# HGRN level products on two halves of the array, 64 keys by 64 queries each

## The chip, the cores and the metric

The kernel runs on one core of one Trainium2 chip. The metric is device time in microseconds of one execution, the median of several. Three runs of the kernel before took 3020.35, 3021.91 and 3026.28 us.

## The reference

One layer of a two-branch sequence model on 1024 latent tokens and 256 context tokens, width 2048, all in float32. A projection `u = h @ w_in` feeds two groups of heads; the change is in group A, a gated linear recurrence in both directions (HGRN2) with 8 heads of 128 key and 128 value dimensions:

```python
# one direction, one chunk; b = cumsum(log f) inside the chunk
o_inter = einsum('bhtk,bhkv->bhtv', qc * exp(b), s)
diff = b[:, :, :, None, :] - b[:, :, None, :, :]
decay = exp(where(mask, diff, -inf))
scores = einsum('bhtk,bhsk,bhtsk->bhts', qc, kc, decay)
o = o_inter + einsum('bhts,bhsv->bhtv', scores, vc)
s_new = exp(b_last)[..., None] * s + einsum('bhsk,bhsv->bhkv', kc * exp(b_last - b), vc)
```

A score of a query t and a key s carries the product of the gates f between the two, another one for each of the 128 key dimensions. The sum of both directions goes through an RMS norm and a gate, is joined with group B (an mLSTM), projected with `w_out`, added to the stream and normalised.

## The kernel before

The program goes through a prelude (modulation of the context), the context, the mLSTM heads, the eight HGRN heads and the output projection. Throughout, TensorE works on projections: a weight tile is brought in by SyncE's queue (`wraw`), split into a rounded part (`whi`, ScalarE, L209) and the rest (`wlo`, VectorE, L210), and multiplied in three matmuls (`mm3`, L218 to L220 or L222 to L224) of operands of the rounded type. `unit_a` makes one projection of 128 channels for 1024 tokens: 96 matmuls of 128 x 512. Between pieces of twelve matmuls it calls `tick()`, which advances side generators: the work of the heads is issued there, in between.

For a head, `hgrn_head` runs five projections (query, two gates, value, output gate). After the third it starts `levels_gen` as a side generator; the sixteen ticks of the last two projections advance it. The tokens of a head lie in 8 chunks of 128. `qq`, `kk` and `ff` hold queries, keys and gate products of both directions, two variants side by side, as 128 partitions (key dimension) by 1024 tokens. The scores `sc` of a chunk, 128 keys by 128 queries, are built by level. First comes one product of all keys and queries (L1101). Then for level lv = 0 to 6, with B = 2^lv, the pairs whose tokens lie in the two halves of the same block of 2B get their score from the product of decayed keys `kms` and decayed queries (L1120), and a predicated copy with the mask of the level (L1133) puts it over what `sc` holds. After the product of a level VectorE multiplies keys (L1124), queries (L1129) and gates (L1132) on to the next level, and ScalarE gathers the next key operand (`kmix`, L1085).

In the kernel before, the work of a level is issued for each half of the chunks (g = 0, 1) at a tick of its own: four matmuls of 128 keys by 128 queries into one PSUM bank (tag `mx`, three banks), then the products and the predicated copy of 128 x 512. All engines run their instructions in program order; a matmul waits for `kms` and `qq`, VectorE's query product waits for the matmuls that read the queries, the predicated copy for the bank. `hout_gen` uses `sc` later, in the projections of the next head.

Of the kernel before, what the change touches and what calls it, by code (L numbers as in the profile page):

```python
# [9 lines left out]
F32 = mybir.dt.float32  # L10
F32R = mybir.dt.float32r
U8 = mybir.dt.uint8
# [9 lines left out]
P = 128  # L22
# [12 lines left out]
def view(t, off, dims):  # L35
    return bass.AP(t.tensor, t.offset + off, [list(t.ap[0])] + [list(d) for d in dims])


class Body:
# [957 lines left out]

    def phase_hgrn(self):
        nc, mp = self.nc, self.mp
        self.lvl = mp.tile([P, 7, P], U8, name="lvl")  # L1000
        lf = mp.tile([P, 7, P], F32, tag="h_sc", name="lvl_f")
        nc.gpsimd.dma_start(out=lf, in_=self.a["k_lvl"])
        nc.gpsimd.tensor_copy(out=self.lvl, in_=lf)
        self.tail = None
        for h in range(HH):
            self.hgrn_head(h)
        self.finish(self.tail)
# [66 lines left out]
    def levels_gen(self, st):  # L1074
        nc, mp = self.nc, self.mp
        V = nc.vector
        T = NT
        qq, kk, ff = st["qq"], st["kk"], st["ff"]
        sc = mp.tile([P, T], F32, tag="h_sc", name=self.nm("h_sc"))
        st["sc"] = sc  # L1080

        def kmix(lv, g):
            B = 1 << lv
            km = mp.tile([P, 512], F32, tag="h_t2", bufs=3, name=self.nm("h_km"))
            nc.scalar.copy(view(km, 0, [[2 * B, 512 // (2 * B)], [B, 2], [1, B]]),  # L1085
                           view(kk, g * 512, [[2 * B, 512 // (2 * B)], [T + B, 2], [1, B]]))
            return km

        kss = []
        for g in range(2):  # L1090
            s = slice(g * 512, (g + 1) * 512)
            ks = mp.tile([P, 512], F32, tag="h_t1", bufs=2, name=self.nm("h_ks"))
            V.tensor_tensor(out=ks, in0=kk[:, 0, s], in1=kk[:, 1, s], op=ALU.add)
            kss.append(ks)
        yield
        pts = []
        for g in range(2):
            pt = self.mx()
            for c in range(4):
                cc = (g * 4 + c) * P  # L1100
                nc.tensor.matmul(pt[:, c * P:(c + 1) * P], kss[g][:, c * P:(c + 1) * P], qq[:, 0, cc:cc + P],  # L1101
                                 start=True, stop=True)
            pts.append(pt)
        kms = [kmix(0, g) for g in range(2)]
        for g in range(2):
            s = slice(g * 512, (g + 1) * 512)
            nc.scalar.copy(sc[:, s], pts[g])
            V.tensor_tensor(out=qq[:, 1, s], in0=qq[:, 0, s], in1=ff[:, 1, s], op=ALU.mult)
            V.tensor_tensor(out=qq[:, 0, s], in0=qq[:, 0, s], in1=ff[:, 0, s], op=ALU.mult)
        yield  # L1110
        for lv in range(7):
            B = 1 << lv
            dims = [[2 * B, P // (2 * B)], [T + B, 2], [1, B]]
            np_ = 512 // (2 * B)
            dimg = [[2 * B, np_], [T + B, 2], [1, B]]
            for g in range(2):
                o = g * 512
                pt = self.mx()
                for c in range(4):
                    nc.tensor.matmul(pt[:, c * P:(c + 1) * P], kms[g][:, c * P:(c + 1) * P],  # L1120
                                     view(qq, o + c * P, dims), start=True, stop=True)
                fk = view(ff, o + T + B, [[2 * B, np_], [-(T + B), 2], [0, B]])
                kv = view(kk, o, dimg)
                V.tensor_tensor(out=kv, in0=kv, in1=fk, op=ALU.mult)  # L1124
                if lv < 6:
                    kms[g] = kmix(lv + 1, g)
                fq = view(ff, o + B, [[2 * B, np_], [T - B, 2], [0, B]])
                qv = view(qq, o, dimg)
                V.tensor_tensor(out=qv, in0=qv, in1=fq, op=ALU.mult)  # L1129
                fe = view(ff, o, [[T, 2], [2 * B, np_]])  # L1130
                fo = view(ff, o + B, [[T, 2], [2 * B, np_]])
                V.tensor_tensor(out=fe, in0=fe, in1=fo, op=ALU.mult)  # L1132
                V.copy_predicated(out=sc[:, o:o + 512].rearrange("p (c t) -> p c t", t=P),  # L1133
                                  mask=view(self.lvl, lv * P, [[0, 4], [1, P]]),
                                  data=pt.rearrange("p (c t) -> p c t", t=P))
                yield

        for d, g in ((0, 0), (1, 1), (0, 1), (1, 0)):
            pt = self.mx()
            for c in range(4):  # L1140
                cc = (g * 4 + c) * P
                nc.tensor.transpose(pt[:, c * P:(c + 1) * P], kk[:, d, cc:cc + P], self.ident)
            nc.scalar.copy(kk[:, d, g * 512:(g + 1) * 512], pt)
            if (d, g) == (1, 1):
                yield
# [176 lines left out]
def constants():  # L1322
    ident = np.eye(P, dtype=np.float32)
    s = np.arange(P)[:, None]
    t = np.arange(P)[None, :]
    lvl = np.stack([((s // (2 * B) == t // (2 * B)) & (s // B != t // B)) for B in (1, 2, 4, 8, 16, 32, 64)],
                   axis=1).astype(np.float32)
    mb = np.stack([np.where(s <= t, 0.0, -1e30), np.where(s >= t, 0.0, -1e30)], axis=1).astype(np.float32)
    comb = np.zeros((4, 2), np.float32)
    comb[0:2, 0] = 1.0  # L1330
    comb[2:4, 1] = 1.0
    sel = np.zeros((32, 2, 64), np.float32)
    for i in range(2):
        for d in range(2):
            for r in range(4):
                sel[(i * 2 + d) * 4 + r, i, d * 32 + r] = 1.0
                sel[16 + (i * 2 + d) * 4 + r, i, d * 32 + r] = 1.0
    return {"k_ident": ident, "k_lvl": lvl, "k_mbias": mb, "k_comb": comb, "k_sel": sel}


def body(tc, nc, **a):
    Body(tc, nc, a).run()


_CONST = constants()
_SHAPES = {"x": (NT, D), "c": (1, D), "ctx": (NC, D), "c_ctx": (D,), "w_mod": (D, 3 * D), "b_mod": (1, 3 * D),
           "w_in": (D, N_IN), "conv_w": (1, 3, 3, D), "conv_b": (1, D), "hg_lb": (2, 2, 1024),
# [21 lines left out]
```

## Time and profile before

| | |
|---|---|
| median of three runs | 3021.91 us |
| the profiled execution | 3019.23 us |
| its span, first to last instruction | 3017.4 us |
| mean granted TensorE clock | 0.990 |
| TensorE matmul busy | 2918.0 us, 97% |
| VectorE, ScalarE busy | 1676.7 us (56%), 970.7 us (32%) |
| product before the levels, first and second head | at 1605.05 and 1742.44 us, 137.4 us apart |

Busy time of an engine is time in which at least one of its instructions runs. A matmul's duration in the trace reaches from its start to the modelled end of its results, so matmuls in a row overlap in the list: what one costs is read from one start to the next. PEld is the load of a matmul's weights, listed apart. The chain of waits is followed back from the last instruction and says what each stretch of the time went to.

### The profile page before, as it was taken

Reading aid. Unit: us, or ns where it says so; the run is one execution under the profiler, and the core shown is the slowest. Engines: PE = TensorE matmul, PEld = TensorE weight load, DVE = VectorE, ACT = ScalarE, POOL = GpSimd, SP = SyncE. Lnnn points to the kernel's source line nnn. Section 1 sums busy time; section 2 is a strip of 40 time slices with the busy share of each in tenths; the row PEclk is TensorE's granted clock in tenths of the full one; section 3 lists DMA queues with packets and bytes.
Section 4 is the critical chain, followed back from the end, with each engine's and each line's share of the span. In section 5 each row is a group of like instructions: output and inputs, shape, how many; then the busy total and the mean of one; then the engine's idle time right before and its main releaser. Section 6 shows DMA issues by size and latency. Waiting matters only on the chain.

```text
span 3017.4 us, 41425 instructions
## 1 busy us (share of the span) xinstructions
PE 2918.0 (97%) x16265; PEld 2502.6 (83%) x16265; DVE 1676.7 (56%) x3154; ACT 970.7 (32%) x1650; POOL 366.0 (12%) x549
## 2 busy tenths in 40 slices
PE   6999998999999999999999999999999999999998
PEld 3689976987897797889778888888888888899876
DVE  7876657563835656383535363544445363634776
ACT  5664545342233223223312222222222232322332
POOL 1011111031012103201210101001010101310111
PEclk9999999999999999999999999999999999999999
DMA  9855642123322323322241112121111212753685
GB/s 321 276 167 169 187 136 68 47 57 106 84 62 72 112 70 79 111 79 75 62 114 42 52 35 58 37 56 51 42 52 42 55 38 58 224 190 118 216 310 178
DMA packets 331843, 325.13 MB, mean 108 GB/s; under 512 B 16512, under 2 KB 285072, under 8 KB 329600
## 3 DMA queue, kind: packets, MB, share of 16 engines
q1 hardware_dynamic: 296848, 243.04, 27.3%
q0 software_dynamic: 30368, 69.52, 8.0%
q10 hardware_dynamic: 4432, 9.91, 0.9%
q8 instruction: 128, 2.10, 0.3%
q14 instruction: 67, 0.55, 0.1%
HBM read 289.37 MB, written 33.05 MB: 107 GB/s over the span
## 4 chain that ended last, share of the span: by engine, by line
PE 75%; DMA 10%; DVE 8%; issue 3%; ACT 2%; POOL 2%; SPq 0%; ACTq 0%; DVEq 0%; POOLq 0%
PE pj L220 16%; PE pj L219 16%; PE pj L218 16%; PE pj L223 5%; PE pj L224 5%; PE pj L222 5%; PE mx L1120 3%; DMA wraw<-in_w_in_dram 2%; DMA am_raw<-in_w_mod_dram 2%; DVE wlo L210 2%; DVE m_acc L855 1%; PE mx L944 1%; DMA m_gt<-d_oz 1%; PE mx L949 1%; PE mx L1162 1%
## 5 line engine op out<-in xcount | busy, mean ns | idle before, releaser
L218 PE MATMUL pj<-hh,whi 128*128 128x512 f32 x2304 | 927.8, 403 | 1.0 <-ACT m_pad L777 1.0
L220 PE MATMUL pj<-hh,wlo 128*128 128x512 f32 x2304 | 902.5, 392 | 6.7 <-DVE wlo L210 6.7
L219 PE MATMUL pj<-hl,whi 128*128 128x512 f32 x2304 | 901.9, 391 | 0.0
L210 DVE TENSOR_TENSOR wlo<-wraw,whi 128x512 fp32r<-128x512 f32 x556 | 391.1, 708 | 664.7 <-ACT whi L209 605.2
L209 ACT CAST whi<-wraw 128x512 fp32r<-128x512 f32 x556 | 340.8, 619 | 889.6 <-PE pj L219 599.9
L220 PEld LDWEIGHTS pj<-hh,wlo 128*128 128x128 f32 x2304 | 434.0, 188 | 102.7 <-DVE wlo L210 10.5
L218 PEld LDWEIGHTS pj<-hh,whi 128*128 128x128 f32 x2304 | 434.6, 189 | 89.0 <-issue 2.5
L219 PEld LDWEIGHTS pj<-hl,whi 128*128 128x128 f32 x2304 | 434.9, 189 | 84.4
L222 PE MATMUL pj<-whi,yh 128*128 128x256 f32 (+1 forms) x768 | 245.9, 320 | 4.4 <-DVE res L1247 4.4
L223 PE MATMUL pj<-wlo,yh 128*128 128x256 f32 (+1 forms) x768 | 246.3, 321 | 2.8 <-DVE wlo L210 2.7
L224 PE MATMUL pj<-whi,yl 128*128 128x256 f32 (+1 forms) x768 | 246.0, 320 | 0.0
L855 DVE SCALAR_TENSOR_TENSOR m_acc<-m_pad,cwt,m_acc 128x512 f32<-128x512 f32 x256 | 184.1, 746 | 3.0
L222 PEld LDWEIGHTS pj<-whi,yh 128*128 128x128 f32 x768 | 147.4, 192 | 14.9 <-DVE res L1247 4.8
L223 PEld LDWEIGHTS pj<-wlo,yh 128*128 128x128 f32 x768 | 147.3, 192 | 13.5 <-DVE wlo L210 3.2
L224 PEld LDWEIGHTS pj<-whi,yl 128*128 128x128 f32 x768 | 147.5, 192 | 10.0
L222 PE MATMUL pj<-whi,hh 128*128 128x256 f32 x512 | 147.4, 289 | 2.0 <-ACT m_pad L777 2.0
L223 PE MATMUL pj<-wlo,hh 128*128 128x256 f32 x512 | 145.8, 285 | 1.4 <-DVE wlo L210 1.4
L224 PE MATMUL pj<-whi,hl 128*128 128x256 f32 x512 | 145.5, 284 | 0.0
L1085 ACT COPY h_km<-h_kk 128x512 f32<-128x512 f32 x112 | 74.5, 665 | 207.1 <-DVE h_kk L1124 147.1
L1120 PEld LDWEIGHTS mx<-h_qq,h_km 128*128 128x128 f32 x896 | 123.6, 191 | 9.3
L1120 PE MATMUL mx<-h_qq,h_km 128*128 128x128 f32 x896 | 126.4, 284 | 0.0
L1193 POOL TENSOR_TENSOR h_ss<-h_ss,nhalf 128x4 f32<-128x4 f32 x16 | 16.6, 1036 | 858.2 <-DVE h_ss L1192 858.2
(308 smaller groups left out, 4340.6 us busy)
## 6 DMA issues: line engine op xcount, KB each, us to landing
wraw<-in_w_in_dram SPq DMA_DIRECT2D x230, 512.0 KB, 3.8
wraw<-in_w_out_dram SPq DMA_DIRECT2D x96, 512.0 KB, 4.7
am_raw<-in_w_mod_dram SPq DMA_DIRECT2D x128, 256.0 KB, 5.9
wraw<-in_w_mod_dram SPq DMA_DIRECT2D x32, 512.0 KB, 3.6
d_y<-yhl POOLq DMA_DIRECT2D x64, 256.0 KB, 3.6
wraw<-in_w_in_dram SPq DMA_DIRECT2D x32, 256.0 KB, 5.9
xt<-in_x_dram SPq DMA_DIRECT2D x8, 1024.0 KB, 6.6
m_bc<-d_rows POOLq DMA_DIRECT2D x64, 128.0 KB, 3.4
```

The lines of the kernel that those rows point to most:

```text
L209: nc.scalar.copy(hi, r)
L210: nc.vector.tensor_tensor(out=lo, in0=r, in1=hi.bitcast(F32), op=ALU.subtract)
L218: mm(o, hi, xh, start=start, stop=False, skip_group_check=True)
L219: mm(o, hi, xl, start=False, stop=False, skip_group_check=True)
L220: mm(o, lo, xh, start=False, stop=stop, skip_group_check=True)
L222: mm(o, xh, hi, start=start, stop=False, skip_group_check=True)
L223: mm(o, xh, lo, start=False, stop=False, skip_group_check=True)
L224: mm(o, xl, hi, start=False, stop=stop, skip_group_check=True)
L855: V.scalar_tensor_tensor(out=acc, in0=src, scalar=wc, in1=acc, op0=ALU.mult, op1=ALU.add)
L944: nc.tensor.matmul(po[:, 0:257], qs[:, j, :], cn[d][:, j, :], start=False, stop=(j == 1))
L1085: nc.scalar.copy(view(km, 0, [[2 * B, 512 // (2 * B)], [B, 2], [1, B]]), view(kk, g * 512, [[2 * B, 512 // (2 * B)], [T + B, 2], [1, B]]))
L1120: nc.tensor.matmul(pt[:, c * P:(c + 1) * P], kms[g][:, c * P:(c + 1) * P], view(qq, o + c * P, dims), start=True, stop=True)
```

## The change

The products of a level are made on two halves of TensorE's columns. Each half holds 64 of a chunk's 128 keys as weights (columns 0 to 63 and 64 to 127, results in PSUM partitions 0 to 63 and 64 to 127) and is fed only the 64 queries that its keys can meet: those of the same half of the chunk up to level 5, at level 6 those of the other half. Both groups of chunks are issued at one tick, 16 matmuls into one bank, and the generator then yields for two ticks. The results are compact: 8 chunks of 64 columns. Levels 0 to 5 are collected in `scd`, 128 x 512, with one predicated copy a level in place of two; after level 5 ScalarE copies its two halves into the diagonal blocks of `sc`, and at level 6 it copies the two off-diagonal blocks out of PSUM. The mask has six levels of 64 columns.

```diff
-        self.lvl = mp.tile([P, 7, P], U8, name="lvl")
+        self.lvl = mp.tile([P, 6, 64], U8, name="lvl")
...
+        TW, NQ = 64, 2
+        scd = mp.tile([P, 8, TW], F32, tag="h_scd", name=self.nm("h_scd"))
+        s3 = sc.rearrange("p (c t) -> p c t", t=P)
+
+        def tiles(kms, rhs, n):
+
+            pt = self.mx()
+            p3 = pt[:, 0:8 * n].rearrange("p (c t) -> p c t", t=n)
+            for c in range(8):
+                cc = (c % 4) * P
+                for j in range(NQ):
+                    q0 = j * TW
+                    nc.tensor.matmul(p3[q0:q0 + TW, c, :], kms[c // 4][:, cc + q0:cc + q0 + TW], rhs(c * P, j),
+                                     start=True, stop=True, skip_group_check=True)
+            return p3
...
-        pts = []
-        for g in range(2):
-            pt = self.mx()
-            for c in range(4):
-                cc = (g * 4 + c) * P
-                nc.tensor.matmul(pt[:, c * P:(c + 1) * P], kss[g][:, c * P:(c + 1) * P], qq[:, 0, cc:cc + P],
-                                 start=True, stop=True)
-            pts.append(pt)
+        p3 = tiles(kss, lambda o, j: qq[:, 0, o + j * TW:o + (j + 1) * TW], TW)
+        nc.scalar.copy(scd, p3)
...
-            nc.scalar.copy(sc[:, s], pts[g])
...
+            if 2 * B <= TW:
+
+                p3 = tiles(kms, lambda o, j: view(qq, o + j * TW, [[2 * B, TW // (2 * B)], [T + B, 2], [1, B]]), TW)
+            else:
+
+                def other(o, j):
+                    t = (j * TW // B ^ 1) * B
+                    return view(qq, o + t + (T if t & B else 0), [[1, B]])
+
+                p3 = tiles(kms, other, B)
             for g in range(2):
                 o = g * 512
-                pt = self.mx()
-                for c in range(4):
-                    nc.tensor.matmul(pt[:, c * P:(c + 1) * P], kms[g][:, c * P:(c + 1) * P],
-                                     view(qq, o + c * P, dims), start=True, stop=True)
...
-                V.copy_predicated(out=sc[:, o:o + 512].rearrange("p (c t) -> p c t", t=P),
-                                  mask=view(self.lvl, lv * P, [[0, 4], [1, P]]),
-                                  data=pt.rearrange("p (c t) -> p c t", t=P))
-                yield
+            if 2 * B <= TW:
+                V.copy_predicated(out=scd, mask=view(self.lvl, lv * TW, [[0, 8], [1, TW]]), data=p3)
+            else:
+                for q0 in range(0, P, B):
+                    t = q0 ^ B
+                    nc.scalar.copy(s3[q0:q0 + B, :, t:t + B], p3[q0:q0 + B])
+            if 2 * B == TW:
+                for q0 in range(0, P, TW):
+                    nc.scalar.copy(s3[q0:q0 + TW, :, q0:q0 + TW], scd[q0:q0 + TW])
+            yield 2
```

TensorE's row at level 0 of the first head, before: `mx` is a bank, `h_km` the key operand of one group of chunks, `pj` the bank of a projection; "x4" are four matmuls, one a chunk.

```order
L220 MATMUL pj_14177<-hh_4687,wlo_14181 128x512
L1120 MATMUL mx_14249<-h_qq_13893,h_km_14227 128x128 x4
L218 MATMUL pj_14177<-hh_4688,whi_14184 128x512
...
L220 MATMUL pj_14177<-hh_4689,wlo_14185 128x512
L1120 MATMUL mx_14272<-h_qq_13893,h_km_14229 128x128 x4
L218 MATMUL pj_14176<-hh_1667,whi_14285 128x512
```

The same place now; L1101 is the matmul in `tiles`, whatever the level.

```order
L220 MATMUL pj_14177<-hh_4687,wlo_14181 128x512
L1101 MATMUL mx_14256<-h_qq_13893,h_km_14236 64x64 x8
L1101 MATMUL mx_14256<-h_qq_13893,h_km_14238 64x64 x8
L218 MATMUL pj_14177<-hh_4688,whi_14184 128x512
...
L220 MATMUL pj_14176<-hh_1668,wlo_14299 128x512
L1101 MATMUL mx_14318<-h_qq_13893,h_km_14274 64x64 x8
```

Both groups of a level stand together, 16 matmuls, and 24 of a projection lie between one level and the next, where twelve lay between the groups.

VectorE's row at level 0 of that head, before: `wlo` is the split of a weight, `h_ff` the gates, `h_kk` the keys.

```order
L1129 TENSOR_TENSOR h_qq_13893<-h_qq_13893,h_ff_13895 128x256x2
L1133 COPY_PREDICATED h_sc_14200<-lvl,mx_14249 128x512
L1132 TENSOR_TENSOR h_ff_13895<-h_ff_13895 128x2x256
L1124 TENSOR_TENSOR h_kk_13894<-h_kk_13894,h_ff_13895 128x256x2
L210 TENSOR_TENSOR wlo_14398<-wraw_14395,whi_14397 128x512
L1129 TENSOR_TENSOR h_qq_13893<-h_qq_13893,h_ff_13895 128x256x2
L1133 COPY_PREDICATED h_sc_14200<-lvl,mx_14272 128x512
L1132 TENSOR_TENSOR h_ff_13895<-h_ff_13895 128x2x256
```

And now (L1143 is the query product, L1138 the key product, L1146 the gates).

```order
L1143 TENSOR_TENSOR h_qq_13893<-h_qq_13893,h_ff_13895 128x256x2
L1148 COPY_PREDICATED h_scd_14201<-lvl,mx_14256 128x512
L1146 TENSOR_TENSOR h_ff_13895<-h_ff_13895 128x2x256
L1138 TENSOR_TENSOR h_kk_13894<-h_kk_13894,h_ff_13895 128x256x2
L1143 TENSOR_TENSOR h_qq_13893<-h_qq_13893,h_ff_13895 128x256x2
L210 TENSOR_TENSOR wlo_14423<-wraw_14420,whi_14422 128x512
L1146 TENSOR_TENSOR h_ff_13895<-h_ff_13895 128x2x256
```

One predicated copy is left, behind the first query product; the second query product no longer stands behind a weight split.

## Rows read from the trace of the kernel before

**Rows 1.** The page: busy time, share of the span and instructions of each engine.

```profile
PE 2918.0 (97%) x16265; PEld 2502.6 (83%) x16265; DVE 1676.7 (56%) x3154; ACT 970.7 (32%) x1650; POOL 366.0 (12%) x549
```

**Rows 2.** One head: window, length, busy PE, PEld, DVE, ACT, POOL, granted clock, DMA.

```profile
1742.40:1879.80 137.40, 137.39 (x723) 117.83 (x722) 64.26 (x114) 34.64 (x70) 8.02 (x10) 1.00 0.18 47
```

**Rows 3.** Chain of waits, that head: shares; start, length, line, passes.

```profile
by line: PE pj L220 26.7%; PE pj L218 26.5%; PE pj L219 26.5%; PE mx L1120 9.8%; PE mx L1162 2.6%; PE mx L1142 1.5%; PE mx L1101 1.4%; PE mx L1180 1.3%; PE mx L1181 1.3%; PE mx L1182 1.3%; PE mx L1071 0.6%; PE mx L1201 0.6%; issue 0.0%
...
1742.20 0.23 PE pj L220
1742.44 1.79 PE mx L1101 x16
...
1746.98 1.33 PE mx L1120 x8
...
1755.14 0.97 PE mx L1120 x8
...
1762.54 0.89 PE mx L1120 x8
```

**Rows 4.** Timeline, one burst of level 2: start, length, engine, line.

```profile
2040.98 1.09 PEld L1120 LDWEIGHTS mx<-h_qq,h_km 128*128 128x128 f32 x8
2041.21 1.06 PE L1120 MATMUL mx<-h_qq,h_km 128*128 128x128 f32 x8
```

**Rows 5.** Timeline, the loads of L568's transposes, 64 moving columns.

```profile
512.85 1.01 PEld L568 LDWEIGHTS mx<-ident,g 64*128 64x128 f32 x15 [2.86 <-issue]
```

**Rows 6.** The instructions of L568: duration ns min/median/max, first and last start, form.

```profile
L568 PEld LDWEIGHTS mx<-ident,g x24: 134/140/222, 512.9 to 514.6; 64*128 64x128 f32 x24
```

**Rows 7.** Timeline, TensorE around L493 (32 rows by 64 columns).

```profile
159.08 0.28 PE L219 MATMUL pj<-ctl,whi 128*128 128x256 f32 x1
159.29 1.07 PE L493 MATMUL mx<-g_sb,selg 32*64 32x256 f32 x4
...
160.52 0.28 PE L218 MATMUL pj<-cth,whi 128*128 128x256 f32 x1
```

**Rows 8.** Timeline, TensorE around L413 (128 rows by one column).

```profile
807.29 0.28 PE L223 MATMUL pj<-wlo,hh 128*128 128x256 f32 x1
807.41 0.28 PE L224 MATMUL pj<-whi,hl 128*128 128x256 f32 x1
807.62 0.59 PE L413 MATMUL mx<-gate_acc,ones 128*1 128x256 f32 x2
...
808.36 0.28 PE L223 MATMUL pj<-wlo,hh 128*128 128x256 f32 x1
```

**Rows 9.** Timeline, TensorE from full width to 32 columns, rounded type.

```profile
45.58 0.28 PE L222 MATMUL pj<-whi,cth 128*128 128x256 f32 x1
45.70 0.28 PE L347 MATMUL pj<-cth,wg 128*32 128x256 f32 x1
```

**Rows 10.** Groups by line and form: count, then busy us and mean ns of one.

```profile
L413 PE MATMUL mx<-gate_acc,ones 128*1 128x256 f32 x16 | 4.7, 377 | 1.3 <-DVE m_gt L975 1.3
...
L1120 PEld LDWEIGHTS mx<-h_qq,h_km 128*128 128x128 f32 x896 | 123.6, 191 | 9.3
L577 PEld LDWEIGHTS pj<-hh,wg 128*32 128x32 f32 x32 | 3.6, 113 | 4.9 <-ACT hh L453 1.9 <-issue 0.3
```

**Rows 11.** Timeline, VectorE at level 0.

```profile
2023.12 1.15 DVE L1129 TENSOR_TENSOR h_qq<-h_qq,h_ff 128x512 f32<-128x512 f32 x1 [0.16 <-PE mx L1120]
2024.12 0.73 DVE L1133 COPY_PREDICATED h_sc<-lvl,mx 128x512 f32<-128x512 uint8 x1
2024.75 0.67 DVE L1132 TENSOR_TENSOR h_ff<-h_ff 128x512 f32<-128x512 f32 x1
2025.45 1.16 DVE L1124 TENSOR_TENSOR h_kk<-h_kk,h_ff 128x512 f32<-128x512 f32 x1
2026.46 0.67 DVE L210 TENSOR_TENSOR wlo<-wraw,whi 128x512 fp32r<-128x512 f32 x1
2027.20 1.16 DVE L1129 TENSOR_TENSOR h_qq<-h_qq,h_ff 128x512 f32<-128x512 f32 x1
```

More of the change, by code (lines that the diff above doesn't have):

```diff
@@ L999, in phase_hgrn @@
         nc, mp = self.nc, self.mp
-        self.lvl = mp.tile([P, 7, P], U8, name="lvl")
-        lf = mp.tile([P, 7, P], F32, tag="h_sc", name="lvl_f")
+        self.lvl = mp.tile([P, 6, 64], U8, name="lvl")
+        lf = mp.tile([P, 6, 64], F32, tag="h_sc", name="lvl_f")
         nc.gpsimd.dma_start(out=lf, in_=self.a["k_lvl"])
@@ L1112, in levels_gen @@
             B = 1 << lv
-            dims = [[2 * B, P // (2 * B)], [T + B, 2], [1, B]]
             np_ = 512 // (2 * B)
             dimg = [[2 * B, np_], [T + B, 2], [1, B]]
+            if 2 * B <= TW:
[5 more added lines that the diff above has]
+                p3 = tiles(kms, other, B)
             for g in range(2):
                 o = g * 512
-                pt = self.mx()
-                for c in range(4):
-                    nc.tensor.matmul(pt[:, c * P:(c + 1) * P], kms[g][:, c * P:(c + 1) * P],
-                                     view(qq, o + c * P, dims), start=True, stop=True)
                 fk = view(ff, o + T + B, [[2 * B, np_], [-(T + B), 2], [0, B]])
@@ L1325, in constants @@
     t = np.arange(P)[None, :]
-    lvl = np.stack([((s // (2 * B) == t // (2 * B)) & (s // B != t // B)) for B in (1, 2, 4, 8, 16, 32, 64)],
+    s0, t0 = s % 64, t[:, 0:64]
+    lvl = np.stack([((s0 // (2 * B) == t0 // (2 * B)) & (s0 // B != t0 // B)) for B in (1, 2, 4, 8, 16, 32)],
                    axis=1).astype(np.float32)
```

## The prediction

> **What bounds the kernel now.** I read the page first: TensorE is busy for 97% of the span [rows 1]. Then the busy time by window for one head of the HGRN phase: in 137.40 us TensorE is busy for 137.39, VectorE for 64.3, ScalarE for 34.6, at a granted clock of 1.00 [rows 2]. Then the chain of waits over the same head: it holds TensorE lines alone, and "issue" has 0.0% [rows 3]. So in this phase every microsecond of TensorE is a microsecond of the kernel, and one that VectorE or ScalarE saves is worth nothing. The chain gives the price of what is changed. A burst of eight passes of the level products costs 1.33 us at level 0, 0.97 at level 1 and 0.89 from level 2 on; the sixteen passes of the product before the levels cost 1.79 [rows 3]. (A float32 matmul runs as two passes: fourteen bursts of four instructions a head are 448, and the trace has 896 [rows 10].) With two bursts a level one head pays 1.79 + 2 x 1.33 + 2 x 0.97 + 10 x 0.89 = 15.29 us, eight heads 122 us, 4% of the span. That is all the change can touch on the path.
>
> **The change part by part.** *Passes.* A burst now holds 16 matmuls, that is 32 passes, of 64 weight columns and 64 moving columns, where the two bursts of a level held 16 passes of 128 and 128. Sixteen passes stand on each half of the array. What such a pass takes is bounded by the 64-column transposes of L568: fifteen loads, one before each, in 1.01 us, the last one 0.14 long, so (1.01 - 0.14) / 14 = 0.062 us from one to the next [rows 5, 6]; against 0.89 / 8 = 0.111 for the present pass [rows 3]. One step of 64 columns is therefore a little dearer than half. What decides is whether a step holds one pass or two.
>
> If one (the halves take turns), an ordinary burst is 32 x 0.062 = 1.98 us, dearer than the 1.78 of the two bursts that it replaces. If two: in one half the second pass of a matmul has to follow its first, but it can stand beside the first pass of the other half, so 32 passes take 17 steps, 17 x 0.062 = 1.05 us. Level 0 reads its queries element by element and pays 1.33 / 8 = 0.166 a pass, half of that 0.083: 2.66 us by turns, 1.41 side by side. Level 1 (0.97 / 8 / 2 = 0.061) goes as an ordinary one.
>
> I take two passes a step. No row of this trace has two matmuls in different columns, so the number of steps is an inference; the price of one step comes from the row in either case. What speaks for it: a load and a stream that share all rows of the array already run side by side (eight loads from 2040.98 on, eight matmuls from 2041.21 on, 0.11 a pair, though one load alone is 0.19 long) [rows 4, 10], so the engine keeps two operands flowing; and the halves share neither weights nor PSUM partitions.
>
> The Trainium skill has a rule on this, "TensorEngine Tiling (Array Packing)", Key Properties: different tiles can load and multiply in parallel; no run here shows it, and by it the sum is the one taken. It has a rule against it too, "TensorE: Matmul & The Clock Gate", Part 3, The mechanism: a load overlaps matmuls in flight only where the row groups differ. The two halves share all rows, so by that rule nothing would overlap and the burst would be the turn-taking one or worse; rows 4, where loads overlap matmuls in the same rows, disagree with it for the whole array.
>
> *Going into the halves and back.* Around a burst the array now changes its division. Two places in the trace show such a change for float32 operands. L413 (one weight column): the matmul before starts at 807.41, and undisturbed ones follow at 0.12, so the next was due at 807.53; the row after next starts at 808.36, so its predecessor had its turn at 808.24. Of these 0.71 us the two passes themselves take 2 x 0.21 (0.59 for both less 0.38 for one), 0.29 is lost [rows 8, 10]. L493 (64 weight columns): due at 159.20, turn at 160.40, four passes of 0.21, 0.36 is lost [rows 7]. I take 0.35, next to the row with 64 columns. The lower bound is nothing: the L347 matmul, 32 columns wide and of the rounded type, follows a full-width one at 0.12 with no loss [rows 9]. Eight bursts a head make 64 round trips, 22 us in all.
>
> The skill's tiling page, Key Properties, says that changing the mode drains the engine; rows 7 and 8 agree, rows 9 do not, and by the rule alone the 0.35 stays.
>
> *Sum.* Seven ordinary bursts of 1.05 + 0.35 = 1.40 and one of 1.41 + 0.35 = 1.76 are 11.56 us a head against 15.29: -3.73, times eight -29.8 us. The profiled execution took 3019.2 us (span 3017.4 and 1.8 around it), so 2989.4. The median of the runs is 2.7 above that execution: 2992.
>
> *VectorE.* Eight of fourteen predicated copies a head go, 0.63 us from start to start [rows 11]: 5 us a head that TensorE covers, priced at zero. The new order must not make a level late, though. After a burst VectorE owes, at level 0, two query products, the copy, a decay product and a key product before the next burst may start: 1.00 + 0.63 + 0.70 + 1.01 + 1.00 = 4.3 us [rows 11], with a weight split of 0.74 in between 5.1. Twenty-four matmuls of 0.23 [rows 3] stand between bursts, 5.5 us. The cover holds by 0.4 us at level 0 and by more than a microsecond at the others, where the products are shorter. If it failed at level 0, that is at most a microsecond a head.
>
> *ScalarE.* One copy of 128 x 512 replaces two, and four of 64 x 512 come at levels 5 and 6: at most two more copies' worth on an engine that works 34.6 us of 137.4 [rows 2]. In its queue the last two wait for the burst of level 6, and behind them stands a split of weights that are needed a projection later: nothing. *DMA:* the level masks are smaller, once; the weight stream is the same in slightly less time.
>
> **The rivals.** *The halves take turns.* TensorE starts passes in program order throughout the trace, and the one row with passes of this length, L568, gives 0.062 each [rows 5]. Then a head costs 7 x (1.98 + 0.35) + 2.66 + 0.35 = 19.32, +4.03, times eight +32: 3051 for the profiled execution, 3054 for the median. Slower. It decides as soon as a pass is more than (15.29 / 8 - 0.35) / 32 = 0.049 us from the next on average.
>
> *The streams overlap, the loads do not.* The mean load is 191 ns for 128 columns and 113 for 32 [rows 10], 0.81 ns a column, so 52 ns for 64. Thirty-two in a row are 1.66 us and hide the rest: 8 x 2.01 = 16.1 a head, +6.5 us: 3028, at the edge of no change.
>
> *Something between*, a pass each 0.046 to 0.049 us: no change, 3020 to 3027.
>
> *No price for the change of division*, as in [rows 9]: 22 us less than the forecast, 2970.
>
> *A price at each swap of halves.* If what [rows 7, 8] show held for every change of half, 15 more half-trips of 0.175 fall in each burst, +2.6 us, some +200 us in all. Nothing in the trace has two halves in turn; the swap leaves the division as it is, so I give it little.
>
> **How the numbers follow.** Overlap with the price 48%, overlap without it 8%, between 7%, loads in a row 9%, turns 24%, price at each swap 4%. The forecast is 2992 us; its own range is 2972 (a tenth of the price) to 3005 (steps of 0.076). A measurement of this kernel tells 0.2%, 6 us, from no change. Faster: 48 + 8 = 56%. Same: the seven and about half of the loads in a row, 11%. Slower: 33%. Since both signs hold much, the range goes from the case without a price, 2968, to the turn-taking one, 3056; outside are the price at each swap and the far ends of these two, some 13%.
>
> **What the profile afterwards would show.** Overlap: in a level burst matmuls start at a mean of about 0.033 us, in pairs, and the chain charges an ordinary burst some 1.4 us; a head lasts about 133.7 us. Turns: one start each 0.062, 2.3 us a burst, a head of 141.4. The price of the division: a gap of about 0.1 us before the first load of a burst and again behind its last matmul; none, and the fourth rival holds. Wrong in another way would be an idle TensorE before a burst that waits for VectorE's query product or ScalarE's key copy, or a head whose time changes by other than eight times the change of a burst.

## The result, and the profile after

The changed kernel takes 2988.65 us in the median of four runs (2986.50 to 2991.62), the kernel before beside it 3023.43 (3020.35 to 3026.28): a ratio of 0.9885, 95% interval 0.9871 to 0.9899. Run again among the experiments it took 2978.34 us, a ratio of 0.9875 (0.9860 to 0.9889). It is faster, by 35 to 39 us; predicted were 30.

The page of the changed kernel [rows 1] has TensorE and its loads shorter, VectorE too, ScalarE a little longer:

```profile
span 2986.3 us, 43392 instructions
PE 2880.9 (96%) x17289; PEld 2444.8 (82%) x17289; DVE 1634.6 (55%) x3090; ACT 986.4 (33%) x1674; POOL 364.8 (12%) x549
```

Busy time by window over the same head as in [rows 2] (the columns are window, length, busy time and instructions of PE, PEld, DVE, ACT and POOL, granted clock, DMA share, GB/s):

```profile
1740.64:1873.22 132.58, 132.50 (x850) 110.28 (x849) 59.16 (x106) 36.58 (x73) 8.04 (x10) 1.00 0.18 49
```

137.40 us have become 132.58, and TensorE is still busy for all but 0.08 of them, at the same clock. The head got shorter because its TensorE work did. The chain of waits over that head, beside [rows 3]:

```profile
by line: PE pj L218 27.8%; PE pj L220 27.2%; PE pj L219 27.0%; PE mx L1101 6.9%; PE mx L1182 2.7%; issue 1.5%; PE mx L1200 1.3%; PE mx L1202 1.3%; PE mx L1201 1.3%; PE mx L1071 0.9%; PE mx L1221 0.7%; PE mx L1162 0.5%; ACT h_z L1058 0.4%; A
...
1744.74 1.49 PE mx L1101 x32
...
1779.77 1.08 PE mx L1101 x32
1780.85 0.43 PE pj L218
```

The level products (now L1101) hold 6.9% of this stretch where the two lines before held 11.2%. (The issue and ScalarE entries are a detour of the chain between 1788.8 and 1792.2, behind the last burst, where TensorE has projections to do.) An ordinary burst, that is one of the levels 2 to 6, has 1.08 us for 32 passes where two had 0.89 each, and the projection matmul behind it takes 0.43 instead of 0.23. To price a burst fully I therefore read it from start to start. This is the timeline (start, duration, engine, line, operation, tile, operands, count) of the burst of level 6, beside [rows 4]:

```profile
1785.90 0.39 PE L219 MATMUL pj<-hl,whi 128*128 128x512 f32 x1
1786.13 0.39 PE L220 MATMUL pj<-hh,wlo 128*128 128x512 f32 x1
1786.44 1.01 PEld L1101 LDWEIGHTS mx<-h_qq,h_km 128*64 128x64 f32 x32 [0.35 <-issue]
1786.45 1.15 PE L1101 MATMUL mx<-h_qq,h_km 128*64 128x64 f32 x32
1787.53 0.50 PE L218 MATMUL pj<-hh,whi 128*128 128x512 f32 x1
1787.86 0.39 PE L219 MATMUL pj<-hl,whi 128*128 128x512 f32 x1
```

Undisturbed projection matmuls start 0.227 us apart (1785.90, 1786.13). From the last one before the burst to the first behind it are 1.40 us, 1.17 too many; from that to the next are 0.33, 0.11 too many. The burst costs 1.28 us. Every cost below is read in this way, to the nanosecond from the starts in the trace, as a median over eight heads. From the start of its first pass to that of its last are 0.93 us; the rest are 0.09 before the burst, 0.15 from the last pass to the next projection matmul, and the 0.11 of that matmul.

That two passes run at once shows in the number of instructions that a window touches: 21 matmuls and 22 loads in 0.62 us from the start of the burst on, ten pairs and a half.

```profile
1786.46:1787.08 0.62, 0.62 (x21) 0.62 (x22) 1.00 0.00 0
```

In the starts of that burst the two passes of a pair, one of the lower and one of the upper half, lie 6 or 7 ns apart, and 58 to 59 ns pass from one pair to the next; only the first pair is followed after some 106. The trace does not name the half of a pass; that a pair has one of each follows from the experiment with one half after the other, below, where passes of one half never start so close.

The load engine shows that something has changed in front of a burst (its idle time before these loads, and what ended it):

```profile
L1101 PEld LDWEIGHTS mx<-h_qq,h_km x1792: 132/138/143, 1612.1 to 2582.8; 128*64 128x64 f32 x200
its engine sat idle before it (us, times) until:
  issue: 19.7, 56
  ACT h_km L1085: 2.8, 8
```

22.5 us in 64 bursts, 0.35 before each. For L1101 and L1120 of the kernel before this list is empty: their loads run beside the last projection matmul [rows 4], while the first load of a burst in halves waits until that matmul has had its turn. These 0.35 are not the price of a burst in halves, though near it in size: for most of them TensorE is still busy with the projection matmul, and only 0.09 are a gap in its work.

### The profile page after: what moved, and what is told of

Same layout as the page of the kernel before. It is cut to its first block, busy times and chain, and to the rows that moved or that the text cites. A ratio compares the mean times of both kernels' runs of the same rounds, so it can differ in the third digit from the quotient of the medians.

```text
span 2986.3 us, 43392 instructions
## 1 busy us (share of the span) xinstructions
PE 2880.9 (96%) x17289; PEld 2444.8 (82%) x17289; DVE 1634.6 (55%) x3090; ACT 986.4 (33%) x1674; POOL 364.8 (12%) x549
## 4 chain that ended last, share of the span: by engine, by line
PE 76%; DVE 8%; DMA 7%; issue 4%; ACT 2%; POOL 2%; ACTq 0%; DVEq 0%; SPq 0%; POOLq 0%
PE pj L218 16%; PE pj L220 16%; PE pj L219 16%; PE pj L223 5%; PE pj L224 5%; PE pj L222 5%; PE mx L1101 2%; DMA wraw<-in_w_in_dram 2%; DVE wlo L210 1%; DVE m_acc L855 1%; PE mx L944 1%; DMA m_gt<-d_oz 1%; PE mx L949 1%; DMA d_y<-yhl 1%; PE mx L1182 1%
## 5 line engine op out<-in xcount | busy, mean ns | idle before, releaser
L218 PE MATMUL pj<-cth,whi 128*128 128x256 f32 x384 | 111.5, 290 | 2.3 <-ACT cth L453 1.9
L220 PE MATMUL pj<-cth,wlo 128*128 128x256 f32 x384 | 110.2, 287 | 2.1 <-DVE wlo L210 1.9
```

The lines of the kernel that those rows point to most:

```text
L218: mm(o, hi, xh, start=start, stop=False, skip_group_check=True)
L220: mm(o, lo, xh, start=False, stop=stop, skip_group_check=True)
```

## The experiments

Kernels that ran on the same chip share the runs of the kernel before (3017 to 3020 us there; the times that the expectations name for the changed kernel start in part from 2989, its first median). A head is the mean distance from one head's first product to the next head's.

| kernel | ratio to before (95%) | head, us | ordinary burst, us |
|---|---|---|---|
| before | 1 | 137.39 | 2 x 0.905 |
| changed | 0.9885 (0.9871 to 0.9899) | 132.58 | 1.281 |
| half by half | 1.0035 (1.0022 to 1.0048) | 138.82 | 2.030 |
| whole array, one tick | 0.9992 (0.9982 to 1.0001) | 137.09 | 1.798 |
| halves, two ticks | 0.9946 (0.9934 to 0.9959) | 135.23 | 2 x 0.814 |
| halves, all queries | 1.0119 (1.0102 to 1.0136) | 142.23 | 2 x 1.225 |
| two and two | one run, 2984.90 us | 132.93 | 1.330 |
| quarters | 0.9797 (0.9783 to 0.9810) | 129.59 | 0.892 |
| quarters, one trip less | 0.9789 (0.9774 to 0.9804) | 129.39 | 0.892 |

**Is it the merge of two bursts, or the halves?** The kernel before with both groups of a level issued at one tick, nothing else:

```diff
+            pts = [self.mx() for g in range(2)]
             for g in range(2):
-                o = g * 512
-                pt = self.mx()
                 for c in range(4):
-                    nc.tensor.matmul(pt[:, c * P:(c + 1) * P], ...
+                    nc.tensor.matmul(pts[g][:, c * P:(c + 1) * P], ...
...
-                yield
+            yield 2
```

> The kernel before, whole array, all 128 queries; only the matmuls of both groups of a level are issued together, one burst of eight matmuls a level instead of two of four, as the changed kernel has it. No halves, no compact results. Theory A (the gain comes from the halves; a burst of the whole array has no change of division to pay for, so that its number does not matter): the time stays within 0.3% of before, 3015 to 3030 us. Rival C (the gain is the merge): about 2989 to 2995. A third way: bursts of 16 passes leave VectorE's work of a level in one lump, TensorE waits for it, and the time rises above 3030.

Measured: 3015.24 us, 0.9992. The last burst of a head:

```profile
1784.97 0.40 PE L220 MATMUL pj<-hh,wlo 128*128 128x512 f32 x1
1785.20 1.95 PE L1119 MATMUL mx<-h_qq,h_km 128*128 128x128 f32 x16
1786.90 0.48 PE L218 MATMUL pj<-hh,whi 128*128 128x512 f32 x1
1787.22 0.40 PE L219 MATMUL pj<-hl,whi 128*128 128x512 f32 x1
```

1.93 - 0.23 + 0.32 - 0.23 = 1.79 for sixteen passes, beside 1.81 for two bursts of eight. Seven bursts fewer make a head 0.30 us shorter. Of that 0.08 lie in the bursts as priced here, 0.10 in the transposes of the keys behind the last level, which stand in other gaps now, and 0.12 in projection matmuls further behind a burst, some of which start up to 9 ns late. Rival C, the merge, has fallen; all but this little of the gain belongs to the halves with their fewer queries.

**What does a trip to the halves cost?** The changed kernel with the groups at two ticks again:

```diff
             for g in range(2):
                 o = g * 512
+                p3 = tiles(kms, rhs, n, p3, range(g * 4, g * 4 + 4))
...
+                if g == 0:
+                    yield
...
-            yield 2
+            yield
```

> The changed kernel with the two groups of a level issued apart again, each a burst of eight matmuls in halves between projections, as the kernel before has its bursts. Same number of matmuls and steps; seven more round trips to the half array and back per head. Theory A (each round trip costs 0.35 us, however many matmuls stand in the burst): 7 x 0.35 x 8 = +19.6 us: 3008. Rival D (the 0.35 us is the level's own, for instance the wait for its data, and no price of a trip): no change, 2989. Rival E (no price for division, the 0.35 is filling and emptying, which at half the burst also is paid once each): the same as A in time, but then before, whose bursts also fill and empty, must show it at its bursts too; the gap from the last projection matmul to the first load of the burst tells them apart.

Measured: 3001.05 us, 0.9946; a head is 2.66 us longer than the changed kernel's, where the price foresaw 2.45. One burst and its surroundings, and the load engine's waits:

```profile
1764.87 0.39 PE L220 MATMUL pj<-hh,wlo 128*128 128x512 f32 x1
1765.19 0.69 PE L1102 MATMUL mx<-h_qq,h_km 128*64 128x64 f32 x16
1765.80 0.50 PE L218 MATMUL pj<-hh,whi 128*128 128x512 f32 x1
1766.14 0.39 PE L219 MATMUL pj<-hl,whi 128*128 128x512 f32 x1
```

```profile
  issue: 39.5, 112
  ACT h_sc L1160: 2.8, 8
```

0.93 - 0.23 + 0.34 - 0.23 = 0.81, and again 0.35 of idle load before each of 120 bursts. A burst of sixteen passes costs 0.814, one of 32 costs 1.281: so eight steps are 0.467, a step 0.058, and what is paid once a trip is 0.814 - 0.467 = 0.347 us. The same sum for the whole array (0.905 and 1.798) gives 0.112 a step and 0.012 once. Level 0, which the fit did not use, agrees: its bursts of 16 and 32 passes cost 1.012 and 1.691, which gives 0.085 a step and 0.333 once. Theory A holds; rival E, that any burst pays for filling and emptying, falls with that 0.012, rival D with the 2.66. Seven trips at 0.347 are 2.43 of the 2.66; the rest is in projection matmuls further behind each burst that start a few ns late, so that a trip costs 2.66 / 7 = 0.38 us all in all.

**Must the two halves stand next to each other in the program?** The changed kernel with all eight lower matmuls of a burst first, then all eight upper:

```diff
-            for c in range(8):
-                cc = (c % 4) * P
-                for j in range(NQ):
-                    q0 = j * TW
+            for j in range(NQ):
+                q0 = j * TW
+                for c in range(8):
+                    cc = (c % 4) * P
```

> The changed kernel, with the sixteen matmuls of a burst in another order: all eight of the lower 64 keys, then all eight of the upper 64 keys, instead of lower and upper in turn. Same matmuls, same number of changes of division, same schedule. Theory A (the gain comes from two neighbouring matmuls of different halves that stream at the same time, and TensorE pairs only what stands next to it): a burst is 32 steps of 0.058 instead of 16, so 7 x 0.93 + one level-0 burst of 16 x 0.084 more per head, about +7.9 us per head, +63 us: 3052 us. Rival B (the two halves have queues of their own, filled some matmuls ahead): the second half starts as soon as it is issued; with a reach of n matmuls the burst is shortened by n steps, and at full reach the time stays at 2989. Rival C (the halves never counted, the gain is only the merge of two bursts into one): 2989, no change.

Measured: 3027.49 us, 1.0035, slower than the kernel before. The burst of level 6, and a window in it as long as the one shown for the changed kernel:

```profile
1797.60 0.39 PE L220 MATMUL pj<-hh,wlo 128*128 128x512 f32 x1
1797.92 1.90 PE L1101 MATMUL mx<-h_qq,h_km 128*64 128x64 f32 x32
1799.75 0.50 PE L218 MATMUL pj<-hh,whi 128*128 128x512 f32 x1
1800.09 0.39 PE L219 MATMUL pj<-hl,whi 128*128 128x512 f32 x1
```

```profile
1798.00:1798.62 0.62, 0.62 (x12) 0.62 (x13) 1.00 0.00 0
```

Twelve matmuls in 0.62 us where there were 21. Passes of one half alone start 58 to 59 ns apart, just as pairs do: the partner in the other half is free. So this kernel is what the rival "the halves take turns" described, and it comes out on the side that it foretold. The 3052 of theory A was too much all the same, with 6.24 us a head in place of 7.9: in the starts, three passes of the upper half begin 4 to 6 ns from one of the lower, where the two blocks meet, and the first of them while three lower passes ahead of it in the program are still due. The burst is 0.347 + 29 x 0.058 = 2.03, three steps short of 32. So it is not true that only neighbours are paired: rival B, which shortens the burst by as many steps as its reach, holds with a reach of three passes.

**Two lower, two upper, in turn:**

```diff
+            for i in range(16):
+                c, j = i // 4 * 2 + i % 2, i // 2 % 2
```

> The changed kernel with the matmuls of a burst in the order lower, lower, upper, upper instead of lower and upper in turn. Theory A with issue strictly in order (a matmul that waits for its half holds back those behind it): a lower and an upper one still meet at every second place, so that all but the first and the last still have a partner: 0.93 to 1.05 us a burst as in turn, 2980 to 2988. Rival B' (a half is only paired with the pass that stands right behind it, pass by pass of one matmul): half of the pairs are lost, 24 steps of 0.054 to 0.062, +0.4 us a burst, 3005 to 3012.

One run: 2984.90 us, and a head 0.36 us longer than in strict turn.

```profile
1781.52 0.39 PE L220 MATMUL pj<-hh,wlo 128*128 128x512 f32 x1
1781.84 1.20 PE L1102 MATMUL mx<-h_qq,h_km 128*64 128x64 f32 x32
1782.97 0.50 PE L218 MATMUL pj<-hh,whi 128*128 128x512 f32 x1
1783.31 0.39 PE L219 MATMUL pj<-hl,whi 128*128 128x512 f32 x1
```

The burst costs 1.33, 0.05 more, about one step: 0.347 + 17 x 0.058. B' falls, and so does the strict order that theory A took, though its range holds the time. If a pass that waits for its half held back all behind it, each block of two matmuls would share only one of its four steps with the next, some 25 steps, 0.46 us more than were measured. In the starts the second pass begins 14 ns after the first, so it is one of the upper half, and in the program at least three lower passes stand between the two. A reach of three passes is enough for this order. What was said ahead of the prediction, that all engines run their instructions in program order, is not true of TensorE here: in halves a pass can start ahead of earlier ones that wait for the other half.

**Halves without fewer queries.** The kernel before, each matmul cut in two halves, each with all 128 queries (shown for the product before the levels; the levels' matmul has the same):

```diff
-                nc.tensor.matmul(pt[:, c * P:(c + 1) * P], kss[g][:, c * P:(c + 1) * P], qq[:, 0, cc:cc + P],
-                                 start=True, stop=True)
+                for q0 in (0, 64):
+                    nc.tensor.matmul(pt[q0:q0 + 64, c * P:(c + 1) * P], kss[g][:, c * P + q0:c * P + q0 + 64],
+                                     qq[:, 0, cc:cc + P], start=True, stop=True, skip_group_check=True)
```

> The kernel before with each matmul of the level products cut into its lower and upper 64 keys, issued in turn; every half keeps all 128 queries, and bursts, masks and copies stay as before. The halves alone, without the shorter streams. Theory A (two neighbours of different halves stream at the same time, and a trip to the halves and back costs 0.34 us more than a burst of the whole array): eight pairs of 0.104 to 0.120 us a burst, the same as the eight passes of 0.112 before, plus 15 trips of 0.34 a head, 8 heads: +41 us, with the pairs 3053 to 3066 beside a before of 3018. Rival A' (overlap works only for streams so short that the next one is already waiting): 16 steps of 0.112 a burst, +0.9 us a burst, over 3150. Rival D (the trip costs nothing of itself): 3018 to 3025.

Measured: 3053.41 us, 1.0119, a head of 142.23.

```profile
1779.86 0.39 PE L220 MATMUL pj<-hh,wlo 128*128 128x512 f32 x1
1780.18 1.09 PE L1122 MATMUL mx<-h_qq,h_km 128*64 128x128 f32 x16
1781.20 0.50 PE L218 MATMUL pj<-hh,whi 128*128 128x512 f32 x1
1781.54 0.40 PE L219 MATMUL pj<-hl,whi 128*128 128x512 f32 x1
```

1.34 - 0.23 + 0.34 - 0.23 = 1.22 a burst, against 0.905 of the whole array: pairs of 128 queries start 109 ns apart, as a single pass of the whole array does at 112, and little but the price of the trip remains. Halving alone loses 36 us; the gain is in the queries that need not be streamed. A' and D fall.

**Quarters.** Four column tiles of 32 keys with 32 queries each; the levels of 32 and of 64 take the other block:

```diff
-        TW, NQ = 64, 2
+        TW, NQ = 32, 4
```

(The mask has five levels of 32 columns to match.)

> The changed kernel with quarters for halves: four column tiles of 32 keys, each with only its 32 queries (the levels of 32 and of 64 take the other block, as the level of 64 does in the changed kernel). 32 matmuls in a burst instead of 16, 64 passes. Theory A1 (a step is set by the time that a tile's queries stream, and four tiles stream side by side): 16 steps of 0.029 to 0.035 instead of 0.058 in seven bursts (the level of 64 keeps its 64 queries), -0.4 us each, -2.6 to -3.3 us per head: 2963 to 2968 us. Theory A2 (a step is set by the weights going in one after another, so many columns at a time, which quarters do not shorten): the same 0.93 us a burst: 2985 to 2992. Theory A3 (a step has a fixed cost of issue for each matmul, about 29 ns, as 16 steps of 58 for 32 passes would also read): 64 passes at 29 ns are 1.87 us a burst, +0.93 x 8 per head, +60 us: 3049.

Measured: 2957.26 us, 0.9797, and 0.9788 (0.9772 to 0.9804) a second time, the fastest kernel here along with the one below. The median lies below A1's 2963 to 2968, which starts from 2989; the head, 2.99 us shorter than in halves, lies inside its 2.6 to 3.3. The head, a window in a burst of 64 passes, and that burst:

```profile
1733.68:1863.28 129.60, 129.52 (x1106) 107.28 (x1105) 57.15 (x105) 38.16 (x79) 8.02 (x10) 1.00 0.18 51
...
1770.12:1770.50 0.38, 0.38 (x44) 0.38 (x47) 1.00 0.00 0
```

```profile
1769.79 0.39 PE L220 MATMUL pj<-hh,wlo 128*128 128x512 f32 x1
1770.10 0.76 PE L1101 MATMUL mx<-h_qq,h_km 128*32 128x32 f32 x64
1770.80 0.50 PE L218 MATMUL pj<-hh,whi 128*128 128x512 f32 x1
1771.13 0.39 PE L219 MATMUL pj<-hl,whi 128*128 128x512 f32 x1
```

44 matmuls in 0.38 us are 0.0086 each; four of them, one a quarter, are a step of 0.034 us. The burst costs 0.892 = 0.347 + 16 x 0.034, that of level 6, which keeps 64 queries, 1.232 = 0.347 + 16 x 0.055; its starts, four within 20 ns and the next four after 56, say the same. A1 holds: with 64 passes in either burst the step goes with the queries, not with the matmuls (A3) or the loads (A2), and the price of the trip does not grow with the number of tiles. Whether the 0.0086 a pass is already near a limit of its own, so that fewer than 32 queries would gain less, these runs do not tell.

**One trip less.** The quarters with a copy of the queries kept, so that the product before the levels and level 0 go out in one burst (the value's tile is taken later, to make room for the copy):

```diff
-        yield
-        p3 = tiles(kss, lambda o, j: qq[:, 0, o + j * TW:o + (j + 1) * TW], TW)
-        nc.scalar.copy(scd, p3)
         kms = [kmix(0, g) for g in range(2)]
...
         yield
+        pk = tiles(kss, lambda o, j: q0[:, o + j * TW:o + (j + 1) * TW], TW)
+        nc.scalar.copy(scd, pk)
```

> The kernel with quarters, with one trip to the divided array less per head: the queries as they come from the projection are kept in a tile of their own, so that the product before the levels and the burst of level 0 can be issued together, seven trips a head instead of eight. Theory A (a trip has a fixed cost of 0.33 us, the matmuls in it cost their steps alone): a head of 129.59 - 0.33 = 129.26 us, eight heads -2.7 us, ratio to before 0.9788 where the quarters alone had 0.9797. Rival V (VectorE's four query products and two key sums now all stand ahead of one burst, 4 to 5 us of work against 5.5 us of projections, and come late): TensorE waits 0.5 us or more a head, no gain or up to 8 us slower.

> The kernel with quarters as it is, run again beside the one with a trip less. 129.59 us a head, ratio to before 0.9797 (0.9783 to 0.981 the first time): 2955 to 2960 us beside a before of 3018.

Measured: 2955.24 us, 0.9789, beside 2955.63 and 0.9788 for the quarters: no difference that the runs could tell. The joined burst costs 1.581 in place of 0.892 + 1.018, so the 0.33 of a trip is saved there. The head is only 0.20 us shorter, though, 129.35 to 129.44 where it had been 129.59 each time. The traces show where most of the other 0.13 went. With the levels one tick earlier, four transposes of the value (L1071, here L1074) no longer stand behind a burst but in a gap of their own, twice a head. First the quarters, then one trip less:

```profile
1750.21 0.76 PE L1101 MATMUL mx<-h_qq,h_km 128*32 128x32 f32 x64
1750.90 0.66 PE L1071 MATMUL mx<-ident,h_vt 128*128 128x128 f32 x4
```

```profile
1752.47 0.39 PE L220 MATMUL pj<-hh,wlo 128*128 128x512 f32 x1
1752.70 0.60 PE L1074 MATMUL mx<-ident,h_vt 128*128 128x128 f32 x4
```

Burst and transposes together cost 1.285; apart they cost 0.892 and 0.443, 0.05 more, so 0.10 a head. Rival V did not come, nor did a gain in the runs.

**The rest of the span.** In its first profile the changed kernel was 38.5 us shorter in eight heads, but only 31.1 in the span.

> The changed kernel as it is, run again beside the others. In its first profile a head was 4.81 us shorter than before, 38.5 us in eight heads, while the span was only 31.1 and the median 34.8 shorter. Theory P (only the heads count, and what lay outside the phase differs from one execution to the next): the ratio to before comes out at 1 - 38.5/3018 = 0.9872, 2980 us, and the profile shows the same 132.57 us a head. Rival Q (the phases outside pay back 4 to 7 us because of the change): 0.9885 to 0.9897 again, 2983 to 2987, and the start of the first head and the stretch after the last are again 3 and 4 us later than before.

> The kernel before as it is, for a second profile beside that of the changed kernel from the same chip. By theory P its first head starts, and its stretch after the last head lasts, as those of the changed kernel within about 3 us; by rival Q they stay 3 and 4 us shorter. 137.4 us a head by both; 3018 us.

The second profiles of the changed kernel and of the kernel before, one head each:

```profile
1731.85:1864.42 132.57, 132.49 (x850) 110.22 (x849) 59.16 (x106) 36.58 (x73) 8.02 (x10) 1.00 0.18 49
```

```profile
1736.10:1873.50 137.40, 137.39 (x721) 117.80 (x720) 64.21 (x114) 34.66 (x70) 8.02 (x10) 1.00 0.18 47
```

Heads repeat to 0.01 us. The start of the first head does not: 1604.9 and 1598.7 in the kernel before, 1608.1 and 1599.3 in the changed one, with nearly the same program ahead of it (the masks are smaller). Changed minus before is now -38.2 us of span (2976.5 and 3014.7), and the ratio 0.9875. From the end of the last head (eight head lengths behind the first start) to the end of the span are 313.4 and 316.9 in the kernel before, 317.6 and 316.6 in the changed one. The 7 us that were missing are what lies ahead of and behind the heads in one execution or another: theory P. The intervals of the ratios are too wide to exclude Q alone; these times speak against it.

## Why the prediction was right

**What bounds the kernel** was right: TensorE's work in the heads is the time, eight times the change of a head is the change of the kernel within what lies outside the heads (-4.81 a head in both profiles). The bursts alone account for -4.75 of it, so that next to nothing is left for the cheaper predicated copies.

**Two passes a step** was the inference on which the sign hung; the range, 2968 to 3056, holds both signs and would have held the turns too, and faster had 56%. The inference holds, with pairs 6 or 7 ns apart. By the rule of the Trainium skill that was weighed against it ("TensorE: Matmul & The Clock Gate", Part 3, The mechanism: a load overlaps matmuls in flight only where the row groups differ) it should not; the measurement decides here, since lower and upper half share all 128 rows and their loads still come in pairs (22 loads in 0.62 us, each 0.138 long). The experiment with one half after the other shows how near the other sign was: the same matmuls in another order are slower than the kernel before.

**The size of the step** was the term that was off. The burst was put at 17 x 0.062 = 1.05. It is 16 steps of 0.058, 0.93: the seventeenth came from letting the first upper pass start beside the second lower one, and it starts beside the first, 6 to 8 ns behind it. The row that gave the 0.062 [rows 5] was near, but not the same thing. Level 0 was put at 1.76 with its trip and costs 1.69 (16 steps of 0.084 where 17 of 0.083 were foreseen); level 1 at 1.40 and costs 1.355. Together the eight bursts cost 10.73 us a head, not 11.56: 0.83 of the difference. On the other side the fifteen bursts of before were read off the chain at 15.29; by starts, with the lengthened projection matmul behind each, they cost 15.48. So -3.73 should have been -4.75. The head shows -4.81. The chain charges an ordinary burst 1.08 and 0.20 in the matmul behind it, not the 1.4 that was to be its sign.

**The price of division** was put at 0.35 beside L493 and L413, and is 0.347, less the 0.012 that a burst of the whole array pays too. The gap of 0.1 us foreseen before the first load and again behind the last matmul is 0.09 and 0.12 (0.15 from the start of the last pass, where a burst of the whole array has 0.03). Not foreseen were two parts: the second pair, 0.05 late, and 0.02 more in the projection matmul behind (0.108 too long after halves, 0.087 after the whole array). That the change of mode drains the engine, as the Trainium skill has it ("TensorEngine Tiling (Array Packing)", Key Properties), agrees with the gap of 0.09 before a burst, which the whole array does not have; [rows 9], where the rounded type pays nothing, stay without an explanation, since no halves of the rounded type were run.

**VectorE's cover** held, by more than was reckoned. After the burst of level 0:

```profile
1746.27 1.16 DVE L1143 TENSOR_TENSOR h_qq<-h_qq,h_ff 128x512 f32<-128x512 f32 x1 [0.33 <-PE mx L1101]
...
1748.61 1.17 DVE L1138 TENSOR_TENSOR h_kk<-h_kk,h_ff 128x512 f32<-128x512 f32 x1
1749.62 1.19 DVE L1143 TENSOR_TENSOR h_qq<-h_qq,h_ff 128x512 f32<-128x512 f32 x1
1750.65 0.68 DVE L210 TENSOR_TENSOR wlo<-wraw,whi 128x512 fp32r<-128x512 f32 x1
...
1751.83 1.23 PE L1101 MATMUL mx<-h_qq,h_km 128*64 128x64 f32 x32
```

The last query product ends at 1750.81, the next burst starts at 1751.83: 1.0 us to spare, in this head and the other seven, where the weight split came behind it; with its 0.68 ahead of it the margin would be 0.3 to 0.4, the 0.4 of the forecast.

**From the head to the median:** -29.8 us were foreseen, -38.5 came in the heads, -34.8 and -38.7 in the two pairs of medians. That 2992 lies only 3 above the first median is luck in part, since errors of both signs met in it: 2992, less 8.7 for the heads, plus 3.7 that the first series lost outside of them, plus 1.5 by which the kernel before came out higher than in the runs shown, is 2988.5. The term that failed is the number and length of the steps, 0.83 us of a head, a sixth of the gain; mechanism, price and sign stood. One rival was summed wrongly: a price of 2.6 us at the swaps of each of 64 bursts is 168 us, which less the gain is 138 above the kernel before, not some 200. No ordinary burst shows such a price, with 58 to 59 ns from pair to pair behind the second.

## What to carry to other kernels

Dividing the array pays where each tile can leave out queries that the whole array had to stream; division by itself only costs, some 0.35 us for every trip between projections here, so put all matmuls of a stage into one trip and issue the tiles in turn, or at most two matmuls of one tile in a row. Price such a burst as (passes of one tile) x (step of its moving columns) + one trip, and take the step from the number of columns, not from the number of tiles. Where one line's end is hidden in the next line's slow start, price from start to start over a stretch of undisturbed neighbours, not by the chain's share of the line.

## What the runs showed of the hardware

The step from pass to pass, of float32, went by the moving columns: 0.034 us for 32 with four tiles at once, 0.055 for 64 with four and 0.058 with one or two, 0.109 to 0.112 for 128 with two tiles or the whole array. Queries read element by element at level 0 cost 0.084 a step for 64 and 0.166 for 128. In an ordinary burst in halves the second pair starts some 106 ns after the first, the others 58 to 59. TensorE started passes of the other half ahead of three still due, and no further in the one order that could show more. A round trip to the halves cost 0.347 us beside 0.012 for a burst of the whole array.
